# Another order of products in pairs of weight sets, with splits, sums and follow-up operations in steps of their own, in a one-core layer kernel

## The chip, the cores and the metric

The kernel runs on one core of a Trainium2 chip. The metric is the device time of one launch in microseconds (us): the median over the runs, 1587.22 us before the change. In the profile PE is TensorE, DVE is VectorE, ACT is ScalarE, POOL is GpSimd and SP is SyncE, which issues the DMAs.

## What is computed

One layer of a streaming encoder on 1024 prompt rows and 32 sample rows (1056 together), all float32, model width 1024:

```python
h = rmsnorm(x, g_mix)
proj = h @ w_in                                   # 1024 x 5120
q, k, v, cb, cc, cx, ga, gc = split(proj)         # 512 each, the gates 1024 each
y_attn = stick_breaking(q, k, v) @ w_attn_out     # 8 heads of 64
conv_out = causal_conv(cc * cx, buf, conv_w)      # width 3, per channel
y_conv = (cb * conv_out) @ w_conv_out
x = x + (sigmoid(ga) * y_attn + sigmoid(gc) * y_conv) @ w_o
x = x + square(relu(rmsnorm(x, g_ffn) @ w_up)) @ w_down    # 1024 x 4096 x 1024
x = x + sigmoid(rmsnorm(x, g_ple) @ w_ple_gate) * (p @ w_ple)
y = rmsnorm(x, g_final)
```

Keys, values and the last convolution rows are outputs too.

## The kernel before

**Products.** Activations lie transposed, 1056 columns of rows of x; a matmul is 128 output channels by 264 columns (a quarter, `TQ`). Each float32 factor is split into a high part (ACT rounds it to a shorter float format) and a low part (DVE subtracts the high part from the original), and a product is three matmuls: high by high, high by low, low by high. So a full product of 512 input channels is 12 matmuls, and an inner one of half that depth is 6.

**Sets.** The input projection (17 sets used by name in `SETS`) and the up projection (16 sets) are cut into sets of 256 output columns, each multiplied by a seven-product scheme in place of eight (Strassen-Winograd): block products A11, S1, S2, S3, S4, A22 and A12 against B11, T1, T2, T3, B22, T4, B21, accumulated in PSUM and read out by ACT or DVE between products. `seven` does one set; `seven_pair` does two sets (a and b), and the products A12 of both at once by a second, inner scheme (`inner_product`, tile names `ps_in...y`). One pair is 330 matmuls. The two PSUM pools (four buffers and two) are taken in rotation through `group`.

**Stages.** First gate columns (plain products, then set i2 by `seven`), pairs (i3,i4) to (i15,i16), attention, the branch projections, the up stage (u0 plain, u1 by `seven`, pairs (u2,u3) to (u14,u15)), the down projection, and the last gated term.

**What sets the order.** Nothing is scheduled by a planner. Every body is a generator, and `run(body)` moves it one step (roughly one product) and then each generator in the list `side` one step. What a step issues is appended to each engine's own in-order queue. So a wait at the head of DVE's queue holds everything behind it, and an operation's place in a queue follows from how many `yield`s stand ahead of it. Side work of a pair is: `prepare` (POOL forms four sums of weight tiles of the next set, then `half_w` splits six operands into `shS/slS`, `shA/slA`), `prepare_inner` (the same for the inner scheme, `whi_...y`, `wlo_...y`, four POOL operations of 128x256), the weight loads (`pair_loads`), and the follow-up of the sets just done. The follow-up of the input stage is `values` (v: difference `dv`, transposes `pt_v` on PE), `keys_or_queries`, `conv_in` (cx: scale, multiply by cc, three taps by `mix`, all 1056 wide) and `conv_gate`. That of the up stage is `up_hooks` (relu, square, stores) and `mid_sums` (four sums `ta`, `tb` for the down stage, stored to memory as `mdT`).

**Within a pair before** the product steps are: A11, S1, S2, S3, S4 of set a (two quarters each, steps 0 to 9); inner A11 and S1 (step 10); A22 of a (11 and 13) with inner S2 and A12 between them (12); inner S3 and S4 (14); S1 of b (15, 16) with inner A22; A11, S2, S3, S4, A22 of b (17 to 26). The chain through the inner buffer `xi` is: product, DVE adds or copies it out into a `p1` tile (L425, L433, L443), the next inner product accumulates on top. Between two of these stand 6 matmuls of another inner product and 12 of a full one.

**Row norms.** `stats_x` squares rows of x on ACT, and `spread` scales an identity by the result (`dg`, DVE, L635) and multiplies it by ones on PE (`pr`, L636), to have 1/rms along the columns. `inner_operands` makes the inner scheme's activation operands (`yiT1x` to `yiT4x`, L283) once in the input stage and once in the up stage.

Of the kernel before, what the change touches and what calls it, by code (L numbers as in the profile page):

```python
# [48 lines left out]
def tile_step(  # L49
# [81 lines left out]
    def group(name, n=TT):  # L131
        p_ = pools[turn[0] % len(pools)]
        turn[0] += 1
        return p_.tile([P, TW], F32, tag="g", name=name)[:, :n]
# [27 lines left out]
    def half_w(src, name):  # L162
        h = wpool[0].tile([P, 4, P], F32R, tag="sh", name=f"sh{name}", bufs=SHB)
        nc.scalar.copy(h, src)  # L164
        l = wpool[0].tile([P, 4, P], F32R, tag="sl", name=f"sl{name}", bufs=SHB)
        dve(l, src, h.bitcast(F32), op=sub)  # L166
        return h, l
# [24 lines left out]
    def prepare(s_, at=(6, 8, 10, 12, 14, 18), shared=None, order=("A11", "S1", "S2", "S3", "S4", "A22")):  # L192
# [12 lines left out]
        def part(k, src):  # L205
            if k == "A11" and not shared:
                w.update(zip(("A11", "A12"), even_odd(load_w(None, 0, KD, f"{s_}", raw=r1))))
            else:
                w[k] = half_w(src, f"{k}_{s_}")
# [10 lines left out]
        for n in range(max(at) + 1):  # L220
            for f in steps.get(n, ()):
                f()
            yield

    def prepare_inner(key, odd):
# [9 lines left out]
        def part(i, c, src):  # L235
            nc.scalar.copy(his[i][:, c, :], src)
            dve(los[i][:, c, :], src, his[i][:, c, :].bitcast(F32), op=sub)
# [5 lines left out]
        part(0, slice(0, 4), r[:, 0:4, :])  # L243
# [6 lines left out]
        pool(a12, a11, a12, op=sub)  # L250
        yield
        part(0, slice(6, 8), a22)
        yield
        yield
        part(1, slice(0, 4), t)
        yield
        part(1, slice(4, 8), r[:, 0:4, :])
        yield

    def inner_operands(name, g, load):  # L260
# [7 lines left out]
        for k in ("T1", "T2", "T3", "T4"):  # L268
            inner_t[k] = blk(f"yi{k}{name}", F32R, [P, 2, 2, TQ])
        for k in range(2):  # L270
            g0, g1 = (g[:, 2 * k + i : 2 * k + i + 1] for i in (1, 5))
            x11, x12, x21, x22 = (raw[k][:, i, j * TQ : j * TQ + TQ] for i in range(2) for j in range(2))
            nc.scalar.activation(x12, x12, AF.Copy, scale=g0)
            mix(x22, x22, g1, x12, sub)
            mix(x12, x11, g0, x12, sub)
            yield
            mix(x11, x11, g0, x22, add)
            mix(x21, x21, g1, x11, sub)
            yield
            for n, (kind, src) in enumerate((("T1", x12), ("T2", x11), ("T3", x22), ("T4", x21))):  # L280
                d = inner_t[kind]
                nc.scalar.copy(d[:, 0, k, :], src)
                dve(d[:, 1, k, :], src, d[:, 0, k, :].bitcast(F32), op=sub)  # L283
                if n % 2:
                    yield

    def inner_product(name, w, b, p_=None):
# [3 lines left out]
        if new:  # L291
            p_ = group(f"ps_in{name}", TQ)
# [8 lines left out]
    def products(name, terms, c, p_=None):  # L301

        new = p_ is None
        if new:
            p_ = group(f"ps_{name}", TQ)
# [62 lines left out]
    def seven_pair(s0, s1, key, m, last, after=({}, {}), meanwhile=int):  # L368
# [5 lines left out]
        x, z = [None] * 2, [None] * 2  # L374

        def product(i, a, b, t, on=None):
            s_ = (s0, s1)[i]
            return products(f"{a}{s_}_{t}", ((ws[s_][a], b),), quarters[t], on)

        def inner(a, b, on=None):  # L380
            return inner_product(f"{a}{key}", ws[key][a], b, on)
# [4 lines left out]
        def sums(i, t):  # L386
            z[t] = product(i, "S1", "T1", t)
            s5 = tile_of("s5", t)
            nc.scalar.copy(s5, z[t])
            return s5  # L390

        def middle(i, s5, u2):
            for t, a, b in q:
                product(i, "S2", "T2", t, x[t])
                u2.append(tile_of("u2", t))
                nc.scalar.copy(u2[t], x[t])
                yield
            for t, a, b in q:
                product(i, "S3", "T3", t, x[t])
                dve(m(i, 1)[:, b], x[t], s5[t], op=sub)  # L400
                yield
            done(i, "22")
            for t, a, b in q:
                product(i, "S4", "B22", t, z[t])
                dve(m(i, 0)[:, b], u2[t], z[t], op=sub)
                yield
            done(i, "12")

        def end(i, t):
            product(i, "A22", "T4", t, x[t])  # L410
            last(m(i, 1), q[t][1], x[t])

        p1 = []
        for t, a, b in q:
            x[t] = product(0, "A11", "B11", t)
            p1.append(tile_of("p1", t))
            nc.scalar.copy(p1[t], x[t])
            yield
        s5 = []
        for t in range(2):  # L420
            s5.append(sums(0, t))
            yield
        yield from middle(0, s5, [])
        xi = inner("A11", "B11")
        dve(p1[0], xi, p1[0], op=add)  # L425
        zi = inner("S1", "T1")
        i5 = tile_of("s5", 2)
        nc.scalar.copy(i5, zi)
        yield
        end(0, 0)  # L430
        yield
        inner("S2", "T2", xi)
        dve(p1[1], xi, p1[1], op=add)  # L433
        c11 = inner("A12", "B21")
        dve(m(0, 0)[:, q[0][1]], c11, p1[0], op=add)
        yield
        end(0, 1)
        done(0, "21")
        meanwhile()
        yield  # L440
        c = [None, tile_of("p1", 2)]
        inner("S3", "T3", xi)
        dve(c[1], xi, i5, op=sub)  # L443
        inner("S4", "B22", zi)
        dve(m(0, 0)[:, q[1][1]], p1[1], zi, op=sub)
        done(0, "11")
        yield
        s5 = [sums(1, 0)]
# [4 lines left out]
        s5.append(sums(1, 1))  # L453
        yield
        for t, a, b in q:
            x[t] = product(1, "A11", "B11", t)
            dve(m(1, 0)[:, a], x[t], c[t], op=add)  # L457
            yield
        done(1, "11")
        yield from middle(1, s5, [])  # L460
        for t in range(2):
            end(1, t)
            yield
            if t == 0:
                done(1, "near")
        done(1, "21")
# [21 lines left out]
    def ahead_of(nm, a, n):  # L488

        return after(n, prepare(f"{nm}{a}", (5, 7, 9, 11, 13, 15), (f"{nm}{a}e", f"{nm}{a}o", 0)))  # L490

    def pair_side(nm, a, b, then=None):

        order = ("S1", "A11", "S2", "S3", "S4", "A22")
        side.append(prepare_inner(f"{nm}{a}y", f"{nm}{a}o"))
        side.append(after(4, prepare(f"{nm}{b}", (4, 6, 8, 11, 14, 16), (f"{nm}{a}e", f"{nm}{a}o", 1), order)))
        if then:
            for n, f in zip((6, 9, 11, 21), pair_loads(nm, *then)):
                side.append(after(n, call(f)))
            side.append(ahead_of(nm, then[1], 17))  # L500
# [74 lines left out]
    def sums_x():  # L575
# [47 lines left out]
        yield  # L623
# [4 lines left out]
    def spread(r9, dst, q0):  # L628

        w = min(3 * P, T - q0 * P)  # L630
        pr = tps.tile([P, 512], F32, tag="tp", name="pr")
        for i in range(q0, q0 + 3):
            n = P if i < 8 else DEC
            dg = cpool.tile([P, P], F32, tag="dg", name="dg", bufs=4)
            nc.vector.tensor_scalar(dg, ident, r9[:, i : i + 1], None, op0=ALU.mult)  # L635
            nc.tensor.matmul(pr[:, (i - q0) * P : (i - q0) * P + n], ones, dg[:, :n], start=True, stop=True)  # L636
        if dst is not None:
            nc.scalar.copy(dst[:, q0 * P : q0 * P + w], pr[:, :w])
        return pr[:, :w]

    def stats_x():
# [12 lines left out]
        for _ in range(3):  # L654
            yield
        for q0 in (0, 3, 6):
            spread(rst, rs, q0)
# [91 lines left out]
    def values(p, m):  # L749
# [6 lines left out]
        nc.scalar.activation(d[:, 0:1], m[:, 0:1], AF.Copy, scale=-1.0)  # L756
        ve = wpool[0].tile([64, 2, 8], F32, tag="ve", name=f"ve{p}", bufs=1)
# [22 lines left out]
    def conv_in(nb, m):  # L780

        scaled(m)
        yield
# [1470 lines left out]
```

## Time and profile before

| | |
|---|---|
| median of 3 runs | 1587.22 us (1586.37 to 1587.33) |
| the profiled execution | 1586.98 us, its span 1585.3 us |
| granted TensorE clock | 0.988 of full |
| busy: PE, DVE | 1527.9 us, 1133.4 us |
| busy: ACT, POOL | 775.2 us, 406.2 us |
| PE busy in 56 to 440 us (set i2 and the input pairs) | 352.85 of 384 us |
| PE busy in 440 to 800 us (attention and branches) | 357.68 of 360 us |
| PE busy in 800 to 1142 us (up) | 337.02 of 342 us |
| PE busy in 1142 to 1472 us (down) | 327.36 of 330 us |

Rows of the waits read "engine, tile, line <- what released it: us in total, times, longest us". Rows of a timeline give the start, the duration, and in brackets the idle time of that engine just before. In rows of windows, "x" counts the instructions that were busy in the stretch and PEclk is the granted clock as a share of full speed. A line number is that of the kernel before.

### The profile page before, as it was taken

What the parts mean: (1) busy time and instruction counts of PE and PEld (TensorE: products, weight loads), DVE (VectorE), ACT (ScalarE), POOL (GpSimd) and SP (SyncE); (2) the same over time, 40 slices, a digit from 0 to 9 for tenths busy, and PEclk for the clock granted to TensorE, in tenths of its full rate; (3) what the DMA queues carried; (4) which work ended last, traced back from release to release, by engine and by line L of the source; (5) the groups of instructions that cost most, each with busy time, mean ns of one, the idle gap of its engine ahead of it and who ended that gap; (6) DMA issues with size and microseconds to landing.
All of it is one profiled execution on the core that took longest, in us unless ns stands there. A gap on an engine that the chain in (4) does not pass through costs nothing.

```text
span 1585.3 us, 29521 instructions
## 1 busy us (share of the span) xinstructions
PE 1527.9 (96%) x11702; PEld 1511.1 (95%) x11702; DVE 1133.4 (71%) x1530; ACT 775.2 (49%) x1466; POOL 406.2 (26%) x350
## 2 busy tenths in 40 slices
PE   8989998998999999999999999999999999999997
PEld 8989998998999999999998999999999999999997
DVE  7565567767679887784669666666667895889866
ACT  6544333433466676433355555555544334434655
POOL 1133242442121112301322333333010121113353
PEclk9999999999999999999999999999999999999999
DMA  6524213431854466434544334444786797683443
GB/s 240 197 94 162 98 63 109 177 132 41 277 149 132 146 215 223 170 101 163 177 171 150 131 141 144 150 149 150 243 304 220 255 339 241 216 274 124 141 131 112
DMA packets 117035, 271.57 MB, mean 171 GB/s; under 512 B 14080, under 2 KB 30080, under 8 KB 116896
## 3 DMA queue, kind: packets, MB, share of 16 engines
q1 hardware_dynamic: 116176, 267.49, 49.8%
q8 instruction: 92, 1.51, 0.4%
q10 hardware_dynamic: 720, 2.19, 0.3%
q14 instruction: 47, 0.39, 0.1%
HBM read 188.89 MB, written 80.73 MB: 170 GB/s over the span
## 4 chain that ended last, share of the span: by engine, by line
PE 77%; DVE 8%; ACT 2%; issue 2%; DMA 1%; SPq 0%; POOL 0%; DVEq 0%; ACTq 0%; POOLq 0%
PE ps_dn L1780 7%; PE ps_dn L1778 7%; PE ps_dn L1779 7%; PE ps_A11u L311 3%; PE ps_A11u L312 3%; PE ps_A11u L313 3%; PE ps_A11i L311 2%; PE ps_A11i L312 2%; PE ps_A11i L313 2%; PE av L1149 2%; PE ps_wo L106 2%; PE ps_wo L107 2%; PE ps_wo L108 2%; PE pa L1130 2%; PE ps_pg L106 2%
## 5 line engine op out<-in xcount | busy, mean ns | idle before, releaser
L1779 PE MATMUL ps_dn<-fl,whi_dn 128*128 128x264 f32 x896 | 254.7, 284 | 1.3 <-DVE fl L1687 1.3
L1780 PE MATMUL ps_dn<-fh,wlo_dn 128*128 128x264 f32 x896 | 254.9, 284 | 0.8 <-DVE wlo_dn L1671 0.8
L1778 PE MATMUL ps_dn<-fh,whi_dn 128*128 128x264 f32 x896 | 254.9, 284 | 0.6 <-ACT whi_dn L1665 0.6
L1779 PEld LDWEIGHTS ps_dn<-fl,whi_dn 128*128 128x128 f32 x896 | 168.6, 188 | 1.5 <-DVE fl L1687 1.5
L1780 PEld LDWEIGHTS ps_dn<-fh,wlo_dn 128*128 128x128 f32 x896 | 168.6, 188 | 1.0 <-DVE wlo_dn L1671 1.0
L1778 PEld LDWEIGHTS ps_dn<-fh,whi_dn 128*128 128x128 f32 x896 | 168.6, 188 | 0.8 <-ACT whi_dn L1665 0.8
L1720 POOL TENSOR_TENSOR c<-c,ssq 128x528 f32<-128x528 f32 x16 | 26.7, 1668 | 241.9 <-DVE c L1787 122.4
L1671 DVE TENSOR_TENSOR wlo_dn<-raw_dn,whi_dn 128x1024 fp32r<-128x1024 f32 x40 | 71.1, 1776 | 24.6 <-ACT whi_dn L1665 24.0
L1094 DVE TENSOR_TENSOR_SCAN r<-r 128x128 f32<-128x128 f32 (+3 forms) x64 | 86.5, 1353 | 2.1 <-POOL r L1087 2.1
L1665 ACT CAST whi_dn<-raw_dn 128x1024 fp32r<-128x1024 f32 x40 | 42.0, 1051 | 93.9 <-PE ps_dn L1779 75.5
L1687 DVE TENSOR_TENSOR fl<-mr,fh 128x1056 fp32r<-128x1056 f32 x56 | 69.8, 1247 | 7.1 <-ACT fh L1682 7.1
L311 PE MATMUL ps_A11i<-T,shS_i 128*128 128x264 f32 x240 | 71.0, 296 | 3.3 <-DVE m_i L457 2.5
L166 DVE TENSOR_TENSOR slS_i<-s_i,shS_i 128x512 fp32r<-128x512 f32 x45 | 40.8, 906 | 44.3 <-ACT shS_i L164 44.0
L311 PE MATMUL ps_A11u<-T,shS_u 128*128 128x264 f32 x240 | 69.2, 288 | 0.8 <-DVE m L457 0.5
L1087 POOL TENSOR_SCALAR_AFFINE_SELECT r<-r 128x128 f32<-128x128 f32 x64 | 26.8, 419 | 168.2 <-ACT r L1080 168.2
L312 PE MATMUL ps_A11i<-T,shS_i 128*128 128x264 f32 x240 | 69.7, 290 | 0.0
L313 PE MATMUL ps_A11i<-T,slS_i 128*128 128x264 f32 x240 | 69.6, 290 | 0.0
L312 PE MATMUL ps_A11u<-T,shS_u 128*128 128x264 f32 x240 | 68.5, 285 | 0.0
L313 PE MATMUL ps_A11u<-T,slS_u 128*128 128x264 f32 x240 | 68.3, 284 | 0.0
L1533 ACT ACTIVATE m<-m 128x528 f32<-128x528 f32 x45 | 29.1, 647 | 75.9 <-DVE m L400 30.4
L1682 ACT CAST fh<-mr 128x1056 fp32r<-128x1056 f32 x56 | 60.0, 1073 | 8.0 <-DMA mr<-mdB 8.0
L1134 DVE TENSOR_TENSOR at<-pa,at 128x512 fp32r<-128x512 f32 (+2 forms) x96 | 51.0, 550 | 16.1 <-ACT at L1133 15.3
(1544 smaller groups left out, 5755.3 us busy)
## 6 DMA issues: line engine op xcount, KB each, us to landing
raw_dn<-in_w_down_dram SPq DMA_DIRECT2D x56, 512.0 KB, 4.6
mr<-mdT SPq DMA_DIRECT2D x32, 528.0 KB, 5.3
mdB<-m SPq DMA_DIRECT2D x48, 264.0 KB, 2.3
mr<-mdB SPq DMA_DIRECT2D x24, 528.0 KB, 6.0
s<-gd SPq DMA_DIRECT2D x16, 528.0 KB, 5.5
mdT<-ta SPq DMA_DIRECT2D x32, 264.0 KB, 2.1
raw_pg<-in_w_ple_gate_dram SPq DMA_DIRECT2D x15, 512.0 KB, 3.5
gd<-sg SPq DMA_DIRECT2D x10, 528.0 KB, 3.3
```

The costliest lines, as they stand in the source:

```text
L106: nc.tensor.matmul(ps, wh, xh[k][:, cols], start=(k == order[0]), stop=False)
L311: nc.tensor.matmul(p_, wh[:, k, :], h, start=new and n == 0, stop=False, **on)
L312: nc.tensor.matmul(p_, wh[:, k, :], l, start=False, stop=False, **on)
L313: nc.tensor.matmul(p_, wl[:, k, :], h, start=False, stop=z, **on)
L1094: nc.vector.tensor_tensor_scan(rev, rev, rev, 1.0, ALU.mult, ALU.bypass)
L1134: nc.vector.tensor_tensor(al, pt[:, :nb, :], ah.bitcast(F32), op=ALU.subtract)
L1671: dve(lo, raw, hi.bitcast(F32), op=sub)
L1682: nc.scalar.copy(h, mraw[v])
L1687: dve(l, mraw.pop(v), opd[v].bitcast(F32), op=sub)
L1778: nc.tensor.matmul(ps, hi[:, j, :], oh, start=j == 0, stop=False)
L1779: nc.tensor.matmul(ps, hi[:, j, :], ol, start=False, stop=False)
L1780: nc.tensor.matmul(ps, lo[:, j, :], oh, start=False, stop=j == NP_ - 1)
```

## The change

The change does five things.

1. `seven_pair` has another order. Set a is unchanged up to S3; then inner A11, S4 of a (both quarters), inner S1, inner S2, A22 of a, A12 (inner), A22, inner S3, S1 of b, inner S4, A11 of b, inner A22, A11, S1, and then S2, S3, S4, A22 of b (25 steps in place of 27). Between two products on `xi` now stand two full products and one inner one (30 matmuls in place of 18). For set b the quarters run in the order 1, 0 for A11, S2, S3 and A22, and the PSUM pool is named (`many` or `few`) in place of the rotation.
2. Splits: the low part of `half_w`, `prepare_inner` and `inner_operands` goes to DVE one step (or more) after the high part to ACT. `prepare_inner` of the next pair starts 17 steps into the pair before, not in its own first steps. `inner_operands` is written out in nine steps and begins at step 5, not 9 (up: 1, not 6).
3. Sums and follow-ups: `conv_in`, `values` (two steps between `dv` and the transposes), keys and queries, `spread` (two steps between `dg` and `pr`, and a step between its three thirds), and the last sums of T4 get further steps.
4. Up stage: `up_hooks` puts relu, square and stores in steps of their own after the product that completes a block; `mid_sums` is issued one sum a step and starts two (for u1 also two) steps after the trigger; `mean_squares` starts 44 steps in, not 14.
5. Loads of the pair after move to steps 6, 8, 10, 19 (before 6, 9, 11, 21), and the work ahead of a stage's end shifts by two steps.

```diff
     def half_w(src, name):
...
-        dve(l, src, h.bitcast(F32), op=sub)
-        return h, l
+        return (h, l), partial(dve, l, src, h.bitcast(F32), op=sub)
...
-        for n in range(max(at) + 1):
+        for n in range(max(at) + 2):
+            while lows:
+                lows.pop()()
             for f in steps.get(n, ()):
...
     def seven_pair(s0, s1, key, m, last, after=({}, {})):
...
+        many, few = pools[0], pools[1]
...
+        for f in (first, second, third, fourth):
+            for t in range(2):
+                f(0, t)
                 yield
+        done(0, "22")
         xi = inner("A11", "B11")
         dve(p1[0], xi, p1[0], op=add)
+        fifth(0, 0)
+        yield
+        fifth(0, 1)
+        done(0, "12")
+        yield
         zi = inner("S1", "T1")
         i5 = tile_of("s5", 2)
         nc.scalar.copy(i5, zi)
-        yield
-        end(0, 0)
-        yield
         inner("S2", "T2", xi)
         dve(p1[1], xi, p1[1], op=add)
-        c11 = inner("A12", "B21")
+        yield
+        sixth(0, 0)
+        yield
+        c11 = inner("A12", "B21", pool_=many)
         dve(m(0, 0)[:, q[0][1]], c11, p1[0], op=add)
-        yield
-        end(0, 1)
+        sixth(0, 1)
         done(0, "21")
-        meanwhile()
         yield
...
         inner("S3", "T3", xi)
         dve(c[1], xi, i5, op=sub)
+        second(1, 0)
+        yield
         inner("S4", "B22", zi)
         dve(m(0, 0)[:, q[1][1]], p1[1], zi, op=sub)
         done(0, "11")
-        yield
-        s5 = [sums(1, 0)]
+        first(1, 1)
         yield
         c[0] = tile_of("p1", 3)
         inner("A22", "T4", xi)
         nc.scalar.copy(c[0], xi)
...
+        first(1, 0)
         done(1, "11")
...
+        second(1, 1, few)
...
     def ahead_of(nm, a, n):
-        return after(n, prepare(f"{nm}{a}", (5, 7, 9, 11, 13, 15), (f"{nm}{a}e", f"{nm}{a}o", 0)))
+        e, o = f"{nm}{a}e", f"{nm}{a}o"
+        return after(n, prepare(f"{nm}{a}", (6, 8, 10, 11, 14, 16), (e, o, 0))), after(n + 3, prepare_inner(f"{nm}{a}y", o))
...
-        side.append(prepare_inner(f"{nm}{a}y", f"{nm}{a}o"))
-        side.append(after(4, prepare(f"{nm}{b}", (4, 6, 8, 11, 14, 16), (f"{nm}{a}e", f"{nm}{a}o", 1), order)))
+        side.append(after(3, prepare(f"{nm}{b}", (4, 6, 8, 10, 13, 15), (f"{nm}{a}e", f"{nm}{a}o", 1), order)))
...
     def spread(r9, dst, q0):
...
+            dgs.append(dg)
+        yield
+        yield
...
     def values(p, m):
...
         nc.scalar.activation(d[:, 0:1], m[:, 0:1], AF.Copy, scale=-1.0)
+        yield
+        yield
...
     def conv_in(nb, m):
         scaled(m)
-        yield
+        for _ in range(2):
+            yield
         u = cst["cc", nb]
         dve(u, u, m, op=ALU.mult)
-        yield
+        for _ in range(2):
+            yield
...
     def mid_sums(s_, m1, m2):
...
         nc.sync.dma_start(md("T1", s_), ta[:, 0, :])
+        yield
         dve(m1[:, b], m2[:, b], m1[:, b], op=sub)
         nc.sync.dma_start(md("T3", s_), m1[:, b])
+        yield
...
     def up_hooks(i, s_, m):
+        def later_(*fs):
+            for f in fs:
+                yield
+                f()
...
         def c11():
-            relu2(m(0), halves[0])
-            done(0, 0, "B11")
+            side.append(later_(partial(relu2, m(0), halves[0]), partial(done, 0, 0, "B11")))
```

**Place 1.** DVE in pair (i9,i10), around the add that takes the first inner product out of PSUM (`p_i` from `ps_inA11i9y`). `slS`, `slA` and `wlo` are low parts, `m_i` with `rs` is a 1056-wide scale, `vecT` rows are the taps of `conv_in`, `cs` and `ce` its two-column corrections. Before:

```order
L405 TENSOR_TENSOR m_i_2804<-u_i_2726,ps_S1i_0_2667 128x264
L166 TENSOR_TENSOR slS_i_2816<-raw_i10r,shS_i_2814 128x512
L405 TENSOR_TENSOR m_i_2804<-u_i_2748,ps_S1i_1_2691 128x264
L155 SCALAR_TENSOR_TENSOR m_i_2541<-m_i_2236,vecT,m_i_2541 128x1055
L799 TENSOR_SCALAR cs_2809<-ce_2808,vecT 128x2
L155 SCALAR_TENSOR_TENSOR cs_2809<-ce_2808,vecT,cs_2809 128x2
L425 TENSOR_TENSOR p_i_2635<-ps_inA11i9y,p_i_2635 128x264
L155 SCALAR_TENSOR_TENSOR m_i_2541<-m_i_2236,vecT,m_i_2541 128x1054
```

The same place after (line numbers of the changed kernel: L441 is the subtraction behind S3, L445 that behind S4, L457 the add in question, L223 a low part, L767 the scale, L829 the multiplication of `conv_in`):

```order
L441 TENSOR_TENSOR m_i_2769<-ps_A11i_0_2636,s_i_2685 128x264
L223 TENSOR_TENSOR slA_i_2751<-raw_i9r,shA_i_2750 128x512
L155 SCALAR_TENSOR_TENSOR m_i_2432<-m_i_2283,vecT,m_i_2432 128x1054
L155 SCALAR_TENSOR_TENSOR m_i_2432<-ce_2729,vecT,cs_2730 128x2
L767 TENSOR_TENSOR m_i_2548<-m_i_2548,rs 128x1056
L441 TENSOR_TENSOR m_i_2769<-ps_A11i_1_2656,s_i_2702 128x264
L457 TENSOR_TENSOR p_i_2649<-ps_inA11i9y,p_i_2649 128x264
L445 TENSOR_TENSOR m_i_2814<-u_i_2724,ps_S1i_0_2672 128x264
L829 TENSOR_TENSOR m_i_2216<-m_i_2216,m_i_2548 128x1056
L223 TENSOR_TENSOR slS_i_2792<-raw_i10r,shS_i_2791 128x512
```

The add now stands ahead of both subtractions behind S4 instead of behind them, and the low part of b's S1 (`raw_i10r`) stands behind it. The first half of the pair still holds the whole follow-up of one cx set.

**Place 2.** DVE around the nine `dg` of the row norms, in pair (i3,i4), with the last splits of `inner_operands` (`yiT1x` to `yiT4x`) ahead of them. Before:

```order
L283 TENSOR_TENSOR yiT1x<-rix_951,yiT1x 128x264
L283 TENSOR_TENSOR yiT2x<-rix_951,yiT2x 128x264
L283 TENSOR_TENSOR yiT3x<-rix_951,yiT3x 128x264
L283 TENSOR_TENSOR yiT4x<-rix_951,yiT4x 128x264
L635 TENSOR_SCALAR dg<-ident,rst 128x128 x9
L166 TENSOR_TENSOR slS_i_1156<-s_i_865,shS_i_1154 128x512
```

After (L671 is `dg`):

```order
L671 TENSOR_SCALAR dg<-ident,rst 128x128 x3
L223 TENSOR_TENSOR slA_i_1179<-raw_i3r,shA_i_1178 128x512
L441 TENSOR_TENSOR m_i_1194<-ps_A11i_1_1084,s_i_1136 128x264
L457 TENSOR_TENSOR p_i_1073<-ps_inA11i3y,p_i_1073 128x264
L445 TENSOR_TENSOR m_i_1242<-u_i_1160,ps_S1i_0_1105 128x264
L223 TENSOR_TENSOR slS_i_1220<-raw_i4r,shS_i_1219 128x512
L445 TENSOR_TENSOR m_i_1242<-u_i_1176,ps_S1i_1_1123 128x264
L671 TENSOR_SCALAR dg<-ident,rst 128x128 x3
```

The inner splits are all further ahead in the queue, and the nine `dg` come in threes with other work between; the matmuls on them are issued two steps after each three.

254 lines of the change are left out of this document (134 added, 120 removed).

## The prediction

> **What bounds the kernel now.** I read the page first, then TensorE's waits by stage, then the clock in windows, then DVE's timeline where the longest wait ends. The profiled execution took 1586.98 us, 0.24 below the median; its span is 1585.3, and 1.7 lie outside.
>
> The first rows of the page:
>
> ```profile
> span 1585.3 us, 29521 instructions
> PE 1527.9 (96%) x11702; PEld 1511.1 (95%) x11702; DVE 1133.4 (71%) x1530; ACT 775.2 (49%) x1466; POOL 406.2 (26%) x350
> ```
>
> PE is the bound, and the change neither removes nor adds a matmul. All it can win is PE's idle time and the time in which PE runs at a lower clock. The waits of PE from 0 to 440 us, and then from 800 to 1145:
>
> ```profile
> PE pt_v L769 <- DVE dv L755: 7.1, 2, 3.6
> PE ps_g L311 <- ACT B L572: 6.1, 1, 6.1
> PE pr L636 <- DVE dg L635: 5.9, 1, 5.9
> PE ps_inA11i9y L296 <- DVE p_i L425: 4.5, 1, 4.5
> PE ps_inA11i15y L296 <- DVE p_i L425: 4.5, 1, 4.5
> PE ps_A11i L311 <- DVE m_i L457: 2.5, 2, 2.1
> PE ps_inS1i15y L298 <- DVE wlo_i15y L237: 1.7, 1, 1.7
> PE ps_inS1i9y L298 <- DVE wlo_i9y L237: 1.7, 1, 1.7
> PE ps_A11i L311 <- ACT u_i L396: 0.8, 2, 0.4
> PE ps_S1i L311 <- ACT shS_i L164: 0.6, 1, 0.6
> PE ps_inA11i5y L296 <- DVE p_i L425: 0.6, 1, 0.6
> PE ps_inA11i11y L296 <- ACT m_i L922: 0.5, 1, 0.5
> ...
> PE ps_inA11u2y L296 <- DVE p_u L425: 2.9, 1, 2.9
> PE ps_inS1u2y L298 <- DVE wlo_u2y L237: 1.0, 1, 1.0
> PE ps_A11u L311 <- DVE m L457: 0.5, 1, 0.5
> ```
>
> All but `ps_g` (the start, which the edits do not touch) are at places that the change edits: 7.1 + 5.9 + 4.5 + 4.5 + 2.5 + 1.7 + 1.7 + 0.8 + 0.6 + 0.6 + 0.5 = 30.4 us in the input stage and 2.9 + 1.0 + 0.5 = 4.4 in the up stage, **34.8 us** together. Attention and the down stage keep their order but for the last steps before down, which I cost at nothing.
>
> A wait also costs what comes after it. Windows behind the long waits, and two undisturbed ones (188:228, 249:257):
>
> ```profile
> 91.00:96.00 5.00, 5.00 (x26) 5.00 (x27) 1.93 (x9) 1.99 (x5) 0.00 (x0) 0.57 0.00 0
> 182.00:188.00 6.00, 6.00 (x31) 6.00 (x30) 2.51 (x6) 2.99 (x8) 0.62 (x1) 0.54 0.23 87
> 188.00:228.00 40.00, 40.00 (x330) 39.81 (x328) 25.71 (x39) 15.55 (x40) 13.74 (x10) 1.00 0.33 107
> 244.00:249.00 5.00, 5.00 (x23) 5.00 (x24) 3.14 (x6) 0.00 (x0) 0.10 (x1) 0.51 0.50 143
> 249.00:257.00 8.00, 8.00 (x68) 8.00 (x67) 6.09 (x6) 3.54 (x7) 6.85 (x4) 1.00 0.04 15
> 324.00:330.00 6.00, 5.98 (x37) 6.00 (x38) 2.30 (x5) 2.63 (x8) 1.00 (x1) 0.72 0.23 87
> 385.00:390.00 5.00, 4.84 (x27) 4.87 (x28) 3.44 (x7) 0.11 (x1) 0.00 (x0) 0.66 0.64 177
> 871.00:877.00 6.00, 6.00 (x28) 6.00 (x29) 5.18 (x8) 1.93 (x6) 1.82 (x2) 0.50 0.26 90
> ```
>
> At clock 1.00, 330 matmuls take 40.0 us, 0.121 each, so a full product of 12 takes 1.45 and an inner one of 6 takes 0.73. In the six cold windows PE is called busy throughout, but runs only 26, 31, 23, 37, 27 and 28 matmuls. The time lost is each window's length less its count times 0.121: 1.9 + 2.2 + 2.2 + 1.5 + 1.7 + 2.6 = **12.1 us**. So the reach of the change is 34.8 + 12.1 = 46.9 us.
>
> The Trainium skill ("TensorE: Matmul & The Clock Gate", sections "HAM oscillation — how this bites in real kernels" and "Why this matters for your kernels") puts the limit at idle gaps of about 3 to 3.4 us. Most of these windows agree, but the one at 871 follows a wait of 2.9 and has a clock of 0.50; by the page's limit that term of 2.6 would not be there to win, and the time below would be 2.6 longer.
>
> **The change part by part.**
>
> *The inner chain.* In pair (i9,i10) PE stood still for 4.5 us because the add L425 was late. DVE's timeline there, and POOL's at its beginning:
>
> ```profile
> 228.82 2.35 DVE L155 SCALAR_TENSOR_TENSOR m_i<-m_i,vecT,m_i 128x1055 f32<-128x1055 f32 x1
> 234.34 0.68 DVE L166 TENSOR_TENSOR slA_i<-raw_i9r,shA_i 128x512 fp32r<-128x512 f32 x1
> 234.94 0.42 DVE L400 TENSOR_TENSOR m_i<-ps_A11i,s_i 128x264 f32<-128x264 f32 x1
> 235.28 1.25 DVE L726 TENSOR_TENSOR m_i<-m_i,rs 128x1056 f32<-128x1056 f32 x1
> 236.45 0.68 DVE L237 TENSOR_TENSOR wlo_i9y<-si_i9y,whi_i9y 128x512 fp32r<-128x512 f32 x1
> 237.39 1.25 DVE L785 TENSOR_TENSOR m_i<-m_i,m_i 128x1056 f32<-128x1056 f32 x1
> 241.68 1.31 DVE L155 SCALAR_TENSOR_TENSOR m_i<-m_i,vecT,m_i 128x1055 f32<-128x1055 f32 x1
> 242.91 0.22 DVE L799 TENSOR_SCALAR cs<-ce,vecT 128x2 f32<-128x2 f32 x1
> 243.30 0.43 DVE L425 TENSOR_TENSOR p_i<-ps_inA11i9y,p_i 128x264 f32<-128x264 f32 x1
> ...
> 228.43 1.63 POOL L222 TENSOR_TENSOR s_i<-raw_i10r,raw_i9e 128x512 f32<-128x512 f32 x1
> 230.13 2.18 POOL L222 TENSOR_TENSOR s_i<-s_i,raw_i9o 128x512 f32<-128x512 f32 x1
> ```
>
> Two things made it late: DVE was full (the taps, 1056-wide scales and inner low parts stood ahead), and the next inner product came only 0.73 + 1.45 = 2.2 us of PE work after the one it adds to. The change takes the three `wlo` splits out of these steps (two at 0.68, the 256-wide one at most that: some 1.8) and puts 30 matmuls, 3.6 us, in between. I sum the changed queue from the first place where DVE must be level with PE: the subtraction behind S3's first quarter can run after 7 products, 10.2 us into the pair. Behind it stand, as the order shows, slA, a tap, its correction, a scale, the second subtraction and the add: 0.42 + 0.68 + 1.31 + 0.22 + 1.25 + 0.42 + 0.43 = 4.7, so the add ends at 14.9. The inner product that needs it starts after ten full and two inner products, 14.5 + 1.5 = 16.0. **The margin is 1.1 us**, and the 4.5 go, with the 1.7 for `wlo` (now split well before the pair begins) and the cold stretch. The cover is thin: three of these rows lengthened as the tap at 228.82 was (2.35 for 1.31) make 18.0 and a wait of 2.0. I keep 0.8 for each of the two such pairs, 1.6. In other pairs DVE is busy 25.7 of 40 us and the same 3.6 cover it; the later adds have 3.6 or 2.9 where A11 of b had 1.5 (L457's 2.5 us).
>
> *Values.* Two steps, 2.9 us, now lie between `dv` and the transposes, against a longest wait of 3.6: at most 0.7 stays each time. I keep 0.7 in all of the 7.1 and none of the cold stretches.
>
> *Row norms.* `dg` comes in threes, behind splits that are issued earlier:
>
> ```profile
> L635 DVE TENSOR_SCALAR dg<-ident,rst 128x128 f32<-128x128 f32 x9 | 3.3, 392 | 0.9 <-PE pr L636 0.3
> ```
>
> Three take 1.2 us and have 2.9. The 5.9 and its cold 1.9 go. But ACT now has the high parts of the inner operands beside the squares of x and the casts of pair (i3,i4). The trace shows no such crowding; its bounds are nothing and the same 7.8 coming back. Nearer to nothing, since ACT is busy 49%: I keep 1.0.
>
> *Up stage.* `wlo_u2y` leaves the pair, and the eight reciprocals of `mean_squares` move to the next one. Against that, a sum written to memory now stands a step or two ahead of the next on DVE, and `tb` may wait for the store of the one before. The stores of these sums between 870 and 1142:
>
> ```profile
> DMA to landing us min/median/max: 2.0/2.1/5.5
> ```
>
> Two steps are 2.9 us: nothing at the median; at worst DVE stands 2.6, with the pair's next subtraction queued behind `tb`, inside 3.6 of cover. I keep 0.7. POOL's operations and SP's loads move one to three steps, and loads that are issued no later than before cost nothing. For the short waits (0.4 to 0.6 each) I keep 1.0.
>
> *The sum.* 46.9 - (1.6 + 0.7 + 1.0 + 0.7 + 1.0) = 46.9 - 5.0 = 41.9 us, and 1587.0 - 41.9 = **1545 us**, which I give for the median too.
>
> **The rivals.**
>
> *Most goes, as summed (chance 0.69).* Its own range is 1537 to 1556: at the low end nothing stays and PE's restarts, a few tenths at each of some 15 waits, go as well; at the high end the kept 5.0 are 16.
>
> *DVE stays the bound in the conv pairs (0.20).* POOL's four sums of the next set now run at the beginning of the pair, as DVE's scales and low parts do, and the rows above show what a meeting does: 2.35 us for a tap that takes 1.31 alone, while POOL's two sums take 1.63 and 2.18. With five lengthened rows the add ends at 20 and PE waits about 4 again. Then the 4.5 + 1.7 of both pairs and their cold 2.2 and 1.7 stay, 16.3, less the 1.6 kept: 1545 + 14.7 = 1560. With the row norms' 7.8 too it is 1568. Against it: the added 1.45 of distance and the 1.8 of splits taken out are certain. The Trainium skill ("SBUF — State Buffer", section "SBUF: two separate sides") says that a DVE operation with two SBUF operands and a GpSimd operation that reads SBUF take turns at one shared pair of ports, and that the loser waits for the whole instruction. By that rule meetings would rather be frequent than rare; the tap agrees.
>
> *DVE is late for the second set (slower, 0.08).* The low parts of set b now go to DVE a step after the high parts, and its products come earlier: S1 of b starts after 12 full and 5 inner products, 21.0 us into the pair. Its low part stands in DVE's queue behind the add, one subtraction and a 1056-wide multiplication: 14.9 + 0.42 + 1.25 + 0.68 = 17.3. The margin is 3.7. If DVE runs later than that in every pair, each of 14 pairs waits at S1 of b. It decides from 42/14 = 3.0 us a pair, a lag of 6.7. With a wait as long as the 4.5 of before and a cold 2.2, 14 x 6.7 = 94 us come back, and the time is 1639. Against it, DVE idles 14 of 40 us in a pair like 188 to 228; for it, from 234 to 244 it hardly stood still.
>
> *The waits only change their names (0.03).* PE would stand at other products for as long as before, 1587. It would need DVE's total work to be the limit, which 71% does not bear out.
>
> **How the numbers follow.** The first case gives the time. The range 1535 to 1568 holds it and the second one. About 0.2%, 3.2 us, is what a measurement of this kernel can tell from no change. Faster by over 0.2%: 0.69 + 0.20 = 0.89; within: 0.03; slower: 0.08.
>
> **What would show it.** PE's waits for L425's, L635's and L755's successors gone, and the granted clock near 1.00 where the cold windows were; the stretch of set i2 and the input pairs, 384 us before, about 344 long (30.4 of waits and 9.5 of cold clock gone). In pair (i9,i10) the add at about 15 us. I would be wrong by the second rival if the add of the conv pairs still ends PE's wait, by the third if a low part of set b (L223 of the changed kernel) heads the list in most pairs, and in the row norms if a cast on ACT does.

## The result and the profile after

The changed kernel takes 1532.22 us (median of 4 runs, 1531.70 to 1533.02) against 1586.80 for the kernel before in the same comparison: a ratio of 0.9657, 95% interval 0.964 to 0.9674. That is 54.6 us faster; the forecast was 42 faster, 1545, in a range of 1535 to 1568. The direction was right and the range missed by 2.8 us.

The page's first rows after:

```profile
span 1530.1 us, 29519 instructions
PE 1508.4 (99%) x11702; PEld 1495.4 (98%) x11702; DVE 1139.1 (74%) x1530; ACT 771.5 (50%) x1466; POOL 417.0 (27%) x350
```

The same matmuls; 19.5 us less PE busy (1527.9 before), because slow matmuls count as busy too, and 35.7 us less PE idle. The span fell by 55.2. By the starts of the first matmul of each stage in the two traces, 42.7 us of it come by the beginning of attention (z at 427.7 before, 385.0 after), 10.6 in the up stage (802.5 to 1140.1 before, 760.0 to 1087.0 after), and about 2 from the start of down on.

PE's waits from 0 to 440 us after; the start of the kernel (`ps_g`) and the first attention block (`pa`) are the only ones over 0.6 (before, eleven groups at edited places came to 30.4):

```profile
PE ps_g L344 <- ACT B L608: 6.9, 1, 6.9
PE pa L1175 <- DVE r L1139: 1.0, 1, 1.0
PE ps_g L345 <- DVE B L155: 0.7, 1, 0.7
PE ps_S1i L346 <- DVE slS_i L223: 0.6, 1, 0.6
...
```

Windows of set i2 and the input pairs, of the up stage, and of the conv pair (i9,i10), the pair that carries the follow-up of a cx set. The clock is 1.00 throughout (0.50 to 0.72 in the cold windows before). In the conv pair DVE is busy 37.8 of 40 us, and PE waits for it once, 0.6 us:

```profile
56.00:385.00 329.00, 327.23 (x2682) 326.20 (x2680) 241.92 (x351) 155.95 (x358) 117.49 (x86) 1.00 0.45 150
760.00:1087.00 327.00, 326.76 (x2677) 325.91 (x2676) 224.87 (x343) 186.24 (x385) 110.65 (x84) 1.00 0.46 160
202.00:242.00 40.00, 39.38 (x323) 39.17 (x322) 37.84 (x47) 17.04 (x39) 18.66 (x12) 1.00 0.22 63
```

DVE's timeline in that pair, which starts at 202.35 on PE:

```profile
204.56 2.34 DVE L767 TENSOR_TENSOR m_i<-m_i,rs 128x1056 f32<-128x1056 f32 x1
206.82 1.78 DVE L223 TENSOR_TENSOR slS_i<-s_i,shS_i 128x512 fp32r<-128x512 f32 x1
208.53 1.24 DVE L829 TENSOR_TENSOR m_i<-m_i,m_i 128x1056 f32<-128x1056 f32 x1
209.70 1.78 DVE L267 TENSOR_TENSOR wlo_i9y<-raw_i9o,whi_i9y 128x512 fp32r<-128x512 f32 x1
...
213.69 0.43 DVE L441 TENSOR_TENSOR m_i<-ps_A11i,s_i 128x264 f32<-128x264 f32 x1
...
217.63 0.42 DVE L457 TENSOR_TENSOR p_i<-ps_inA11i9y,p_i 128x264 f32<-128x264 f32 x1
```

The add ends at 218.05, 15.7 us into the pair, and the inner product that needs it starts at 218.40, at 16.05: a margin of 0.35 us, where the forecast had 14.9, 16.0 and 1.1. Three rows were lengthened by 1.1 us each (2.34, 1.78, 1.78), but ahead of the subtraction at 213.69, where some of the lag was worked off.

### The profile page after: what moved, and what is told of

The parts are those of the page before. It is cut to its first block, busy times and chain, and to the rows that moved or that the text cites. A ratio compares the mean times of both kernels' runs of the same rounds, so it can differ in the third digit from the quotient of the medians.

```text
span 1530.1 us, 29519 instructions
## 1 busy us (share of the span) xinstructions
PE 1508.4 (99%) x11702; PEld 1495.4 (98%) x11702; DVE 1139.1 (74%) x1530; ACT 771.5 (50%) x1466; POOL 417.0 (27%) x350
## 4 chain that ended last, share of the span: by engine, by line
PE 78%; DVE 2%; ACT 2%; issue 1%; DMA 1%; POOL 0%; DVEq 0%; SPq 0%; POOLq 0%
PE ps_dn L1826 7%; PE ps_dn L1824 7%; PE ps_dn L1825 7%; PE ps_A11u L345 4%; PE ps_A11u L344 4%; PE ps_A11u L346 4%; PE av L1194 2%; PE ps_wo L106 2%; PE ps_wo L107 2%; PE ps_wo L108 2%; PE ps_S1u L345 2%; PE ps_S1u L344 2%; PE ps_S1u L346 2%; PE pa L1175 2%; PE ps_pg L106 2%; PE ps_pg L107 2%
## 5 line engine op out<-in xcount | busy, mean ns | idle before, releaser
L344 PE MATMUL ps_A11i<-T,shS_i 128*128 128x264 f32 x240 | 68.6, 286 | 0.3 <-ACT u_i L437 0.3
L345 PE MATMUL ps_A11i<-T,shS_i 128*128 128x264 f32 x240 | 68.5, 285 | 0.0
L108 PE MATMUL ps_wo<-mh,wlo_wo 128*128 128x352 f32 x192 | 62.0, 323 | 0.0
L107 PE MATMUL ps_wo<-ml,whi_wo 128*128 128x352 f32 x192 | 62.0, 323 | 0.0
```

The source lines that it names most:

```text
L107: nc.tensor.matmul(ps, wh, xl[k][:, cols], start=False, stop=False)
L108: nc.tensor.matmul(ps, wl, xh[k][:, cols], start=False, stop=(k == order[-1]))
L344: nc.tensor.matmul(p_, wh[:, k, :], h, start=new and n == 0, stop=False, **on)
L345: nc.tensor.matmul(p_, wh[:, k, :], l, start=False, stop=False, **on)
```

## Experiments: what one stop costs

The first question was the size of the reach: 46.9 us by the forecast, at least 54.6 in fact. A kernel with stops of chosen length gives their price.

**A ladder of stops.**

```diff
+    LADDER = {"u2": 11, "u4": 13, "u6": 15, "u8": 17, "u10": 19, "u12": 22, "u14": 26}
+    pad = cpool.tile([P, 264], F32, name="pad")
...
         xi = inner("A11", "B11")
+        for _ in range(LADDER.get(s0, 0)):
+            dve(pad, pad, pad, op=add)
         dve(p1[0], xi, p1[0], op=add)
```

> The changed kernel with idle adds on a scratch tile ahead of the inner chain's first add in the seven pairs of the up stage: 11, 13, 15, 17, 19, 22 and 26 of them, about 0.35 us each, so that PE stops for about 0.4, 1.1, 1.8, 2.5, 3.2, 4.3 and 5.7 us there. It gives the price of one stop against its length. Theory: each stop costs its length in the row of PE plus 0.16 us, and from about 2.9 us on also 2 to 2.6 us of slow matmuls behind it; sum about 19 + 1 + 3 x 2.3 = 27 us, so 1559 us. Rival: the clock drops only beyond 3.4 us, so two of the seven have a slow stretch, 1557 us; second rival: short stops cost no more than their length and none a slow stretch, 1551 us.

It took 1574.75 us (one run). The adds were longer than expected, so the stops were too; what counts is each stop beside its cost. PE's waits from 750 to 1150:

```profile
PE ps_inA11u14y L332 <- DVE p_u L462: 8.5, 1, 8.5
PE ps_inA11u12y L332 <- DVE p_u L462: 6.7, 1, 6.7
PE ps_inA11u10y L332 <- DVE p_u L462: 5.3, 1, 5.3
PE ps_inA11u8y L332 <- DVE p_u L462: 4.3, 1, 4.3
PE ps_inA11u6y L332 <- DVE p_u L462: 3.4, 1, 3.4
PE ps_inA11u2y L332 <- DVE p_u L462: 3.0, 1, 3.0
PE ps_inA11u4y L332 <- DVE p_u L462: 1.9, 1, 1.9
```

Of the expectations the second rival falls: stops of 3.4 us and more have a slow stretch, so the edge lies above 3.0 in this run and at or below 3.4. Against the changed kernel, from one pair's first inner product to the next (for the last pair, to the start of down), the stops of 1.9, 3.0, 3.4, 4.3, 5.3, 6.7 and 8.5 made the pair longer by 2.2, 3.3, 5.0, 6.7, 7.7, 8.4 and 10.6 us: 0.3 more than the row for the first two, and 1.6 to 2.4 more from 3.4 on. The row of a wait is short of the cost by some tenths even without a slow stretch. Windows behind the stops of u2, u6 and u8 in the ladder, then behind the 2.5 and the 2.9 alone in the next kernel, then behind single stops of three kernels further below (only the inner splits, 1.9; only the order, 2.5; low parts at once, 2.9):

```profile
822.00:827.00 5.00, 5.00 (x41) 5.00 (x42) 3.13 (x7) 2.45 (x5) 0.00 (x0) 1.00 0.25 67
910.00:915.00 5.00, 5.00 (x31) 5.00 (x32) 2.68 (x7) 1.95 (x4) 0.00 (x0) 0.71 0.28 87
956.00:961.00 5.00, 5.00 (x24) 5.00 (x25) 2.15 (x5) 1.38 (x3) 0.00 (x0) 0.53 0.27 70
...
904.00:909.00 5.00, 5.00 (x42) 5.00 (x43) 3.08 (x7) 2.48 (x5) 0.10 (x1) 1.00 0.34 109
947.00:952.00 5.00, 4.79 (x28) 4.79 (x29) 2.72 (x7) 1.64 (x4) 0.00 (x0) 0.69 0.18 59
...
283.50:288.50 5.00, 5.00 (x29) 5.00 (x30) 1.60 (x5) 1.22 (x3) 0.00 (x0) 0.66 1.00 342
179.50:184.50 5.00, 5.00 (x29) 5.00 (x30) 1.76 (x4) 2.32 (x6) 0.96 (x1) 0.66 0.27 105
259.00:264.00 5.00, 5.00 (x41) 5.00 (x42) 3.19 (x6) 2.87 (x6) 0.00 (x0) 1.00 0.88 313
```

**One stop or two.** The scratch adds stand ahead of the first and of the second add of the chain, (first, second):

```diff
+    LADDER = {"u6": (13, 0), "u8": (14, 0), "u10": (11, 13), "u12": (11, 14), "u14": (13, 13)}
```

> The changed kernel with scratch adds ahead of the first or second add of the inner chain in five pairs of the up stage: one stop of about 2.5 us (u6), one of 3.0 (u8), two about 4 us apart of 1.5 and 2.4 (u10), of 1.5 and 2.9 (u12), and of 2.4 and 2.4 (u14). In the ladder a single stop of 3.0 was followed by no slow matmul and one of 3.4 by 1.4 us of loss, whereas before the change one of 2.9 that followed another of 1.0 had 2.6. Theory (what counts is idle time summed over some microseconds, not one gap): u6 and u8 lose their stop and 0.2 each, u10 to u14 lose 2 us more than their stops: about 2.7 + 3.2 + 4.3 + 4.8 + 5.2 + 3 x 2 = 26 us, 1558 us. Rival (one gap of over 3 us decides, and the one of before was at its edge): no slow stretch in any, 20 us, 1552 us.

1558.3 us (one run), the time of the theory, but not for its reason. Alone, the stop of 2.5 lengthened its pair by 2.7 at clock 1.00, and that of 2.9 by 4.5 at 0.69. So a single 2.9 can bring a slow stretch, while the ladder's 3.0 did not. With two stops (1.5 and 2.9, 1.5 and 3.4, 2.5 and 2.9) the pairs were 6.5, 7.0 and 7.4 longer, about 2 more than the stops. Neither theory is settled by this. The last three windows above widen the zone: with no other stop of 0.3 us or more in the 8 us before, a stop of 1.9 and one of 2.5 were followed by a clock of 0.66, and one of 2.9 kept 1.00. In the input stage (from 60 us on) and the up stage of all fourteen traces, each of the 22 stops of 3.1 us and more was followed by a clock of 0.71 or less over the next 5 us. What decides between 1.9 and 3.0 us is not shown.

## Experiments: one part undone, one part alone

Each of the next five kernels is the changed one with one part as before.

**Order of products undone**: `seven_pair` as before.

> The changed kernel with the product order and the rotating pools of before in seven_pair, all else as changed. Theory (distance on PE): each stop of before whose cause is the 1.45 or 2.2 us between two products on one buffer comes back: up to 1 us at the inner chain of the two conv pairs, 2.1 + 0.4 us at the first add of set b's A11, and 0.2 to 0.6 in each of the other pairs, some 0.5 us for each of 12, so 1539 to 1543 us in place of 1532. Rival (DVE's fullness was the cause and the other edits have mended it): only the 0.5 a pair or less comes back, 1533 to 1536. A second rival: the inner chain's distance is what counted, 4.5 us and a cold clock come back in both conv pairs: 1550 or more.

1538.35 us, ratio 0.9698 (0.9683 to 0.9712): 6.1 of the gain are lost. The sum is just under the theory's range, but it is made up otherwise. The 0.5 us for each of twelve pairs did not come (the up stage is 0.8 longer in all), and the inner chain waits only 0.3. What decides is one stop, 4.5 where the theory had 2.1: at the first add of b's A11 (L490) in pair (i9,i10), behind `conv_gate`, with slow matmuls after it:

```profile
226.54 2.35 DVE L764 TENSOR_TENSOR m_i<-m_i,rs 128x1056 f32<-128x1056 f32 x1
228.93 2.23 DVE L851 TENSOR_TENSOR m_i<-m_i,m_i 128x1056 f32<-128x1056 f32 x1
231.09 2.33 DVE L764 TENSOR_TENSOR m_i<-m_i,rs 128x1056 f32<-128x1056 f32 x1
233.45 2.20 DVE L851 TENSOR_TENSOR m_i<-m_i,m_i 128x1056 f32<-128x1056 f32 x1
235.58 0.42 DVE L490 TENSOR_TENSOR m_i<-ps_A11i,p_i 128x264 f32<-128x264 f32 x1
```

Each of the four runs beside one of POOL's sums of the next set, two of which read:

```profile
227.86 2.19 POOL L225 TENSOR_TENSOR raw_i11r<-raw_i11r 128x512 f32<-128x512 f32 x1
230.12 2.17 POOL L225 TENSOR_TENSOR s_i<-raw_i11r,raw_i11e 128x512 f32<-128x512 f32 x1
```

All four take 2.2 to 2.35 us where 1.25 is the usual, 4.1 us more in sum. In the input stages of all fourteen traces, each of the 133 operations of this form (two operands of 128x1056) that took over 1.5 us overlapped POOL's work by more than 0.3, and the 188 without such an overlap took 1.24 to 1.26; 67 overlapped and were not so lengthened. No kernel was run without POOL's sums, so POOL as the cause is a reading of these rows and not a test. It is the forecast's second rival, long rows in the conv pairs, in another step of the pair. In the changed kernel three of these four are as long (2.35, 2.00, 2.35), and PE does not wait: the new order has distance enough there.

**The inner splits late**: `prepare_inner` at `after(n + 9, ...)` instead of `after(n + 3, ...)`.

> The changed kernel with prepare_inner six steps later, so that its splits and POOL's four sums for it fall into steps 0 to 9 of the pair that needs them, about as before. Theory: the add of the conv pairs ended 0.35 us before PE needed it, and about 1.8 us of splits, or 3 with POOL in the way, now stand ahead of it: PE waits 1.5 to 3 us in each of the two conv pairs, and 0 in the others: 1535 to 1540 us. Rival (the longer distance covers it): 1532 to 1534 us.

1549.77 us, 0.9771 (0.9755 to 0.9788): 17.5 lost, the most of any part and above both theories. The add waits 1.1, near the 1.5 expected, but the larger wait is one that I had not named, for the low part itself, since inner S2 now follows inner S1 directly:

```profile
PE ps_inA11i9y L331 <- DVE wlo_i9y L267: 2.5, 1, 2.5
PE ps_inA11i9y L329 <- DVE p_i L457: 1.1, 1, 1.1
```

The two stops of this pair end 3 us apart, and the clock behind the second is 0.66 (226 to 231 us). A 2.5 alone kept 1.00 in the run with one stop or two and had 0.66 in the one with only the order, so this does not show that idle time adds up over some microseconds. The up pairs, too, each lose 0.4 to 0.55.

**Follow-ups undone**: `conv_in`, `values`, keys and queries, `stats_x`, `spread` as before.

> The changed kernel with conv_in, values, keys and queries, stats_x and spread stepped as before. Theory: the stops at the transposes (3.6 us twice) and at the row norms (5.9 us) come back with a cold clock behind each, 5.2 us for each of the first and 8 for the other: 1532 + 18 = 1550 us, 1546 to 1554. Rival (DVE's queue is emptier there now, by the product order and the splits): half of it, 1538 to 1543 us.

1546.70 us, 0.9752 (0.9738 to 0.9767): 14.5 lost, just inside the theory's range. The stop at the row norms is 5.1 (`dg`), those at the transposes come to 3.7 rather than 7.1, and 4.2, which the theory did not have, appear at copies of u by ACT. A lower clock follows the row norms (0.67 from 87.5 to 92.5 us).

**Up stage undone**: `up_hooks`, `mid_sums` and the start of `mean_squares` as before.

> The changed kernel with up_hooks, mid_sums and the start of mean_squares as before (its reciprocals fall into pair (u2,u3) again). Theory: the new product order alone gives the up stage its cover, so nearly all of its gain stays: 1532 to 1535 us, the up stage 327 to 330 us long. Rival: the up stage's 10.5 us came from these steps: 1538 to 1543 us, with 0.5 us a pair and the stops of pair (u2,u3) back.

1544.16 us, 0.9738 (0.9724 to 0.9753): 11.9 lost, the rival's answer and a little more. The stretch up to the first inner product of pair (u2,u3) is 7.2 us longer. Its largest stop, 3.1, is for a low part (`slS_u`, at S2) that stands in DVE's queue behind four sums issued at once and a split; the reciprocals, which the expectation named, come only after it. Some 1.8 of the 7.2 only moved: the matmuls of the mean squares, which the changed kernel has in the next pair. The last pairs are 0.7 to 1.0 longer each, and the start of down 3.3.

**Low parts at once**: `half_w` and `prepare_inner` issue the subtraction in the step of the cast.

> The changed kernel with the low part of half_w and of prepare_inner handed to DVE in the same step as the high part to ACT, all else as changed. Theory: DVE then stands 0.7 to 2 us at the head of its queue for each of some 15 casts a pair, but works that off within the pair; only the conv pairs, with 0.35 us of margin, wait 1 to 2 us each: 1533 to 1537 us. Rival (the step between high and low is what keeps the queue moving): a wait of 0.5 us or more in each of 14 pairs, 1540 us or more.

1541.88 us, 0.9726 (0.9708 to 0.9743): 9.7 lost. That is the rival's size, but not its place: the up pairs hardly change (0.2 at most), and the input stage loses nearly all of it. The two conv pairs wait 1.6 and 1.2, as the theory had it, but most of the wait of PE's weight loads is for ACT's copies, not for the low parts:

```profile
PEld ps_A11i L346 <- ACT u_i L439: 6.7, 5, 3.1
PEld ps_inA11i9y L331 <- DVE p_i L459: 1.6, 1, 1.6
```

The other way round, the kernel before with parts added.

**Only the order**: the new `seven_pair` with its pools.

> The kernel before with the new seven_pair alone (25 steps, named pools); splits, follow-ups, inner operands and up_hooks as before. Theory (the parts need each other): the order takes away the stops of 2.5, 0.5 and about 0.45 a pair at the first add of A11 (some 8 us) and shortens the two of 4.5, but the transposes, the row norms and the low parts of the inner operands, which stand at the same distance from their users, stay: 1587 - 15 = 1572 us, 1565 to 1580. Rival (the order is the change, all else is small): 1545 us or less. Second rival: as the inner products come earlier for splits that are not moved, new waits on wlo eat it: 1583 to 1595.

1574.18 us, 0.9927 (0.991 to 0.9943): 11.8 faster, as the theory has it. The stops at transposes (6.1) and row norms (6.1) stay; those of the conv pairs fall from 4.7 to 2.6, with a clock of 0.66 behind the one in pair (i9,i10) all the same.

**Only the inner splits early.**

```diff
+        return after(n, prepare(...)), after(n + 3, prepare_inner(f"{nm}{a}y", o))
...
-        side.append(prepare_inner(f"{nm}{a}y", f"{nm}{a}o"))
```

> The kernel before with prepare_inner started in the pair before (its POOL sums and splits leave the first ten steps), the product order and all else as before. Theory: the 1.9 us waits on wlo (two in the input stage, 1.2 in up) go with their restarts, and with 1.8 us less on DVE ahead of the add the stop of 4.7 at the inner chain falls to 2 to 3 us in each conv pair, so that the clock does not drop: 1587 - (5.0 + 3 x 2 + 2 x 2) = 1572 us, 1566 to 1577. Rival (its place only counts with the new order): 1582 to 1587.

1583.50 us, 0.9989 (0.9979 to 0.9998): 2.4 faster, the rival's answer. The waits on `wlo` are gone from the list and those at the inner chain of the conv pairs fell to 2.1 and 1.9, both as the theory had it, but PE now waits 10.8 us for ACT's copies of u (1.2 before).

**Only the follow-ups.**

> The kernel before with the new steps of conv_in, values, keys and queries, stats_x and spread alone. Undoing them in the changed kernel cost 14.5 us. Theory: the stops at the transposes (7.5) go with both slow stretches (3.7), and at the row norms (6.1) at most half goes, as the splits of the inner operands still stand ahead of dg; in the conv pairs the stops stay within 1 us of 4.7: 1587 - 14 = 1573 us, 1569 to 1577. Rival (as for the other parts, it pays only with the rest): 1580 us or more.

1571.66 us, 0.9914 (0.99 to 0.9929): 13.7 faster, as the theory has it, though its 1 us at the conv pairs was wrong: there the stop of 4.7 fell to 1.8, and the one at the first add of b's A11 in pair (i9,i10) grew from 2.4 to 5.1.

**Order and inner splits together.**

> The kernel before with the new seven_pair and with prepare_inner started in the pair before: two parts together, splits at once, follow-ups and the up stage's hooks as before. The order alone gave 12 us and the move alone 2.4, while taking the move out of the changed kernel cost 17.5. Theory (each opens what the other needs: the order gives distance, the move takes work off DVE ahead of the inner chain): more than their sum, 1587 - 22 = 1564 us, 1559 to 1568, with no stop left at the inner chain of the conv pairs and those at the transposes, the row norms and the start of down still there. Rival (they only add): 1571 to 1574 us. Second rival (the splits at once fill ACT and DVE, as when only the move was made): 1574 or more.

1579.81 us, 0.9962 (0.9951 to 0.9974): 5.7 faster, less than the order alone. My theory, that the two help each other, fell; the second rival (ACT and DVE in each other's way) holds. The trace shows where. PE's weight loads first, then ACT's timeline in the conv pair (i9,i10) and the matmul that waits there:

```profile
PEld ps_A11i L311 <- ACT u_i L404: 12.2, 4, 3.6
```

```profile
229.03 1.18 ACT L796 ACTIVATE m_i<-m_i,vecT 128x1056 f32<-128x1056 f32 x1 [4.32 <-DVE m_i L788]
...
231.17 0.65 ACT L404 COPY u_i<-ps_A11i 128x264 f32<-128x264 f32 x2
...
231.59 0.59 PE L311 MATMUL ps_A11i<-T,shS_i 128*128 128x264 f32 x1 [2.91 <-ACT u_i L404]
```

ACT has the first tap of `conv_in` at the head of its queue and stands 4.3 us until DVE has multiplied; the copies of u, which PE needs before it can add to that PSUM buffer, are behind it, and PE stands 2.9. PE waits for ACT, ACT for DVE. The same comes once more, in pair (i15,i16). The other two of the four waits, 2.2 and 3.4, stand behind the casts of keys (`kh`), for which ACT waits 2.8 and 4.0 us in the same way.

**The same with `conv_in` in two steps.**

> The kernel before with the new seven_pair, prepare_inner in the pair before, and conv_in with two steps (not one) between scale, multiplication and taps. Without the last, ACT stood up to 6.6 us at its first tap for DVE's multiplication, 21.7 us in the four conv sets, with the copies of u behind it, for which PE waited 12.2 us. Theory (ACT's queue was blocked from the front): ACT's wait falls below 8 us and PE's 12.2 below 4, with the slow matmuls behind them gone: 1580 - 8 - 4 = 1568 us, 1563 to 1571. Rival (DVE's work in these pairs is simply too much): ACT's wait moves to another operation and the time stays at 1576 to 1580 us.

1573.56 us, 0.9923 (0.9907 to 0.994): 6.2 better, not the 12 of the theory, whose range it misses by 2.6. ACT's wait at the tap fell as expected, PE's wait less so. ACT's waits at the tap in 60 to 430 us, before the edit and after it:

```profile
ACT m_i L796 <- DVE m_i L788: 21.7, 4, 6.6
```

```profile
ACT m_i L798 <- DVE m_i L789: 6.9, 4, 2.7
```

After the edit, the weight loads' wait and one of ACT's stops at `kh`:

```profile
PEld ps_A11i L311 <- ACT u_i L404: 7.8, 4, 3.6
...
273.12 1.05 ACT L739 CAST kh<-m_i 128x1024 fp32r<-128x1024 f32 x1 [3.99 <-DVE m_i L729]
```

PE's two waits behind the tap fell from 2.9 to 0.7 us each. The two behind the casts of keys, which this edit leaves alone, stayed at 2.2 and 3.4. So the theory had the mechanism right and gave all of the 12.2 to the tap, where half of it belonged to another operation of the same kind.

**What follows.** Alone, the order, the inner splits and the follow-ups give 11.8, 2.4 and 13.7 us; taken out of the whole, order, inner splits, follow-ups, up stage and deferred low parts cost 6.1, 17.5, 14.5, 11.9 and 9.7, together 59.7 of a gain of 54.6. (These come from separate comparisons, in which the kernel before took 1585.3 to 1586.8 us.) The parts are not terms of a sum: the inner splits are worth 2.4 alone and 17.5 in the whole, and the order gives less with them than without. Shown for the tap is why: a piece that waits for another engine at the head of an in-order queue holds what PE needs from it. That each part removes one of several such pieces fits the other rows, but was not shown part by part.

## Why the prediction was right or wrong

*The bound (PE, its idle time and its clock): right.* What was to be won was won where it was looked for: the stretch that was to shrink from 384 us to about 344 lost the 42.7, which leaves 341.3.

*The reach: mis-sized; this is the step that failed.* I summed PE's waits, 34.8 us, and took them for the whole cost of the stops; the restarts, a few tenths each, I put at the low end of a range (1537) and not in the sum. In these rows a matmul lasts 0.28 us and the next starts 0.12 after it, so PE's idle time is counted only from 0.16 us after the next one could have started. The longest stop of pair (i9,i10) before, 4.77 from start to start and so 4.65 long, has 4.49:

```profile
239.10 0.28 PE L313 MATMUL ps_A11i<-T,slA_i 128*128 128x264 f32 x1
243.87 0.56 PE L296 MATMUL ps_inA11i9y<-yiT2x,whi_i9y 128*128 128x264 f32 x1 [4.49 <-DVE p_i L425]
```

The weight loads stood longer at the same places, and at some that PE's rows do not list. The kernel before, by the waits of PEld:

```profile
PEld pt_v L769 <- issue: 7.5, 2, 3.7
PEld ps_inA11i9y L296 <- issue: 4.7, 1, 4.7
PEld ps_A11i L311 <- DVE m_i L457: 2.9, 2, 2.4
PEld ps_A11u L311 <- DVE m L457: 1.9, 5, 0.7
PEld ps_dn L1779 <- DVE fl L1687: 1.5, 1, 1.5
PEld ps_A11i L311 <- ACT u_i L396: 1.2, 2, 0.6
PEld ps_dn L1780 <- DVE wlo_dn L1671: 1.0, 1, 1.0
```

Each stop is 0.2 longer (4.7 for 4.5, 3.7 for 3.6), the stops of the up pairs at L457 are five and 1.9 us, not one of 0.5, and the start of down has 1.5 + 1.0 + 0.8. Summed over the same places, these rows give 39.3, not 34.8; a wait of 0.6 at set i2 that I left out and the 3.3 of down make it 43.2. The ladder bears this out from the other side: a stop costs 0.3 more than PE's row without any slow stretch.

*The start of down, costed at nothing: wrong by about 2 us*, and with the up stage as before it is 3.3 (the run with that part undone).

*The cold stretches, 12.1: right in kind.* The clock is 1.00 there after, and the ladder puts 1.6 to 2.4 on each long stop, where I had 1.5 to 2.6.

*What was kept, 5.0: too much.* By the weight loads some 2.9 of touched waits remain (the largest 0.8), and none at the transposes, the row norms or the inner chains, for which I kept 0.7, 1.0 and 1.6. With 43.2 + 12.1 - 2.9, and 0.8 more at the kernel's untouched start, the sum is 51.6, against 55.2 of span. By the starts of the matmuls, counting what goes beyond 0.121 us each, the other 3.6 are about 1.7 in the up stage and 1.1 in the input stage, in gaps that these rows do not list and slightly longer slow stretches, and 1.1 between the first matmul and 56 us, where nothing was edited.

*The inner chain: right and near its edge*, a margin of 0.35 where 1.1 was summed. *The stores of the up sums:* DVE did stand at `tb` for them, 6.5 us in all and 3.0 at the longest (2.6 was the bound), and PE did not wait for it:

```profile
DVE tb L1596 <- DMA mdT<-m: 6.5, 3, 3.0
```

*The rivals.* What the second one builds on was there, long rows where POOL works, but the rows fell on a place with slack. In the run with the old order they decided. The slower case did not come: one wait of 0.6 us for a low part of set b, at S4 in pair (i9,i10), is all there is of it.

## What to carry to other kernels

Size what a kernel on the TensorE bound can win from the weight loads' waits or from the starts of its matmuls, not from PE's idle rows: a stop here cost 0.2 to 0.3 us more than its row, and small ones that recur in each pair were not listed at all. With in-order queues, look for the instruction at a queue's head that waits for another engine and ask what is behind it: one more step on either side of the multiplication in `conv_in` gave 6.2 us back, where the multiplication itself takes 1.25. Parts of such a change do not add, so take each out of the whole as well as trying it alone. And look up an operation's place in the queue before laying a stop to it: the reciprocals, and half of the wait that was put down to the tap, belonged elsewhere.

## What was new of the hardware

Every stop of PE of 3.1 us or more in the input stage (from 60 us on) and the up stage of these traces was followed by a lower clock (0.50 to 0.71 over the next 5 us). Between 1.9 and 3.0 it went either way: 1.00 after single stops of 2.5, 2.9 and 3.0, but 0.66 after one of 1.9 and one of 2.5, and 0.69 after one of 2.9. The Trainium skill ("TensorE: Matmul & The Clock Gate", section "Why this matters for your kernels") names about 3 us as the gap to avoid; the traces agree for stops above it, and show that staying below it was not always enough. In the ladder a longer stop cost no more beyond its own length: 1.6 to 2.4 us for 3.4 to 8.5. Operations of 1.25 us on DVE took 2.2 to 2.35 four times in a row beside POOL's sums, which took up to 2.2 for 1.3; none of that form was so long without POOL at work.
